# Summing the four strips of a modulation product: transpositions and additions instead of products with a selection matrix

## The chip, the cores and the metric

The kernel runs on one core of a Trainium2 chip. Its engines work beside each other: TensorE (PE in the rows; its loads of the stationary operand are PEld), VectorE (DVE), ScalarE (ACT), GpSimd (POOL) and SyncE (SP), whose queue issues nearly all transfers from device memory. [...] The metric is the device time of one execution in microseconds (us); the kernel before was timed in three runs.

## The reference

One layer of a diffusion backbone, for 512 latent tokens and 128 context tokens that share all weights. What bears on this case is the modulation: a conditioning vector of 1,024 values for each of the two token groups is multiplied by a matrix of 1,024 by 6,144, and the result is six vectors of 1,024 for each group (shift, scale and gate, twice). Everything behind the first norm needs the first two of them.

```python
mod = (jax.nn.silu(cond) @ w_ada + b_ada)[..., None, :]
sh1, sc1, g1, sh2, sc2, g2 = jnp.split(mod, 6, axis=-1)
h = _rmsnorm(x, norm1_g) * (1 + sc1) + sh1
mq, mk, mv, mo, gates, q_lat, kv_lat, k_rope = _split_cols(h @ w_in, IN_SIZES)
...
x = x + g1 * (jnp.concatenate([hm, ha], axis=-1) @ w_out)
h2 = _rmsnorm(x, norm2_g) * (1 + sc2) + sh2
x = x + g2 * (jnp.square(jax.nn.relu(h2 @ w_mlp_up)) @ w_mlp_down)
```

## The kernel before

Tokens lie along the free dimension, 640 of them, features along the 128 partitions. Large products are made in three terms (a high part and a low part of each operand) so that they keep float32 accuracy. Order of the work: norm of x, modulation and the input projection for the values of the first head group (`mv`), key and value latents (`kv`), query latents (`ql`), then per head `qk` and `mo`, the mLSTM, the query up projection (`qu`), the attention, the output projection, and the two feed-forward products, which fill the second half. The order on each engine is set by a scheduler that moves instructions by a timeline of its own, so a changed instruction can move others near it.

The modulation is made in twelve **visits**, each of 512 of the 6,144 columns for both groups. Four (`ada_first`, g from 0 to 3) stand at the start and give shift1 and scale1; eight (`ada_steps`) are spread over the `ql` and `qk` products (visits 5 to 8) and over `qu` (visits 9 to 12), where their weights come in chunks `st` of 1 MB from `in_w_ada`. A chunk has one of two buffers, so SyncE issues the next one when the products of an older one are done.

In a visit, `strips` (line 389) runs 32 products of 32 output rows each, four side by side in the array, one for each strip j. Strip j takes half of the 1,024 inputs (k = j // 2) and half of the columns (n = j % 2); rows 0 and 1 of a strip hold the two groups, the other 30 are zero. So each result is the sum of two strips. `mod_cols` forms that sum and turns it from rows into columns: ScalarE copies the 128 x 256 block out of PSUM (line 394), two products with a 128 x 4 selection matrix of ones and zeros (line 397; the matrix is the last four columns of `small`) sum the strips and move features onto partitions, and two VectorE instructions add the bias and write `modT` (line 400).

`modT` is then read by the norm (lines 475 to 482, per pair of feature blocks: `acol`, `h`, and the high and low parts `hh` and `hl`, which are the operands of `mv`), and later by the second norm and the gates. Near visits 9 to 12 the attention starts: `Tq` and `Tk` (lines 928 and 937) are transpositions of the first head's query and key, `mx` and `mr` (lines 947 and 954) its row maxima and their row, and `st` (line 982) its first scores. Line 488 and its neighbours are the three terms of a product (`mm3`).

Of the kernel before, what the change touches and what calls it, by code (L numbers as in the profile page):

```python
# [14 lines left out]
ALU = mybir.AluOpType  # L15
# [4 lines left out]
P = 128  # L20
# [34 lines left out]
def hybrid_layer(ctx: ExitStack, tc: tile.TileContext, d, o):  # L55
    nc = tc.nc
    V, S, G, PE = nc.vector, nc.scalar, nc.gpsimd, nc.tensor
# [23 lines left out]
    def view(t, off, *shape):  # L81
        n = int(np.prod(shape))
        v = t[:, off:off + n]
        if len(shape) == 1:
            return v
        names = "abcd"[:len(shape)]
        return v.rearrange("p (%s) -> p %s" % (" ".join(names), " ".join(names)), **dict(zip(names, shape)))

    def Tt(name, dt=F32, n=T):
        t = tp.tile([P, 646], dt, tag="t", name=name)  # L90
        return t[:, :n]
# [7 lines left out]
    def psD(name):  # L99
        return psd.tile([P, 1024], F32, tag="d", name=name)  # L100

    def psS(name):
        return pss.tile([P, 512], F32, tag="s", name=name)
# [96 lines left out]
    def wget(key, ahead=3):  # L200
        i = state["get"]
        assert chunks[i][0] == key, (chunks[i][0], key)
        wsplit(i + 1)
        wdma(i + 4)
        wsplit(i + ahead)
        state["get"] += 1
        return ready.pop(i)
# [120 lines left out]
    ident = const.tile([P, P], F32, name="ident")  # L328
# [8 lines left out]
    small = const.tile([P, 98], F32, name="small")  # L337
# [3 lines left out]
    cond, bada = small[:, 25:41], small[:, 41:89]  # L341
# [41 lines left out]
    modT = const.tile([P, 48, 2], F32, name="modT")  # L383

    def strips(ps, n, q, w):

        for j in range(4):
            k, c = j // 2, slice((j % 2) * n, (j % 2) * n + n)
            PE.matmul(ps[32 * j:32 * j + 32, 0:n], lhsT=sz[:, 2 * q + k, :], rhs=w[:, k, c], start=q == 0, stop=q == 3, tile_position=(0, 32 * j))  # L389

    def mod_cols(n, c0, step, ps):

        rows, pt = Tt(f"m4{c0}", n=n), ps[:, 256:512]
        S.copy(rows, ps[:, 0:n])
        nb = n // P
        for m in range(nb):
            PE.matmul(pt[:, m * 4:m * 4 + 4], lhsT=rows[:, m * P:(m + 1) * P], rhs=small[:, 94:98], start=True, stop=True)
        for k in range(2):
            c = slice(c0 + k * step, c0 + k * step + nb)
            V.tensor_tensor(out=modT[:, c, :], in0=pt[:, 0:4 * nb].rearrange("p (m n c) -> p m n c", n=2, c=2)[:, :, k],  # L400
                            in1=bada[:, c].unsqueeze(2).broadcast_to([P, nb, 2]), op=ALU.add)

    fps = {}

    def ada_first(g, q0=0, q1=4):

        if q0 == 0:
            fps[g] = psS(f"ada{g}")
        for q in range(q0, q1):
            strips(fps[g], 256, q, adu[2 * g + q // 2][:, 2 * (q % 2):2 * (q % 2) + 2])  # L410
        if q1 == 4:
            mod_cols(256, 2 * g, 8, fps[g])

    ada_key = iter(ada_order)
    ada_ps = {}

    def ada_steps(n, ahead=3):
        for _ in range(n):
            nb, q = next(ada_key)
            if q == 0:  # L420
                ada_ps[0] = psS(f"ada{nb}")
            w = view(wget(("ada", nb, q), ahead), 0, 2, 2, 512)
            for k in range(2):
                strips(ada_ps[0], 256, 2 * q + k, w[:, k])
            if q == 1:
                mod_cols(256, 4 * nb, 2, ada_ps[0])


    def rstd_bc(pc, name):
# [15 lines left out]
    for k in range(0, KT, 2):  # L445
# [4 lines left out]
        for i in range(NT):  # L450
            c = 5 * k + 2 * i
            PE.matmul(pc[:, c:c + 2], lhsT=sq[0][:, i * P:(i + 1) * P], rhs=mean_col, start=True, stop=True)
    ms1 = sm("ms1", [P, NT], bufs=1)
    V.tensor_reduce(out=ms1, in_=pc[:, 0:5 * KT].rearrange("p (j i b) -> p i b j", i=NT, b=2)[:, :, 0], axis=AX.X, op=ALU.add)
    ada_first(0, 0, 2)
    ada_first(0, 2, 4)
    rb = rstd_bc(ms1, "n1")
    acol1 = const.tile([P, KT, 2], F32, name="acol1")
# [7 lines left out]
    for g in range(4):  # L466
        if g:
            ada_first(g)
        if g == 1:
            rbs = Tt("rb1")  # L470
            S.copy(rbs[:, 0:TL], rb[0])
            S.copy(rbs[:, TL:T], rb[1])
            rb = rbs[:, 0:TL], rbs[:, TL:T]
        c2 = slice(2 * g, 2 * g + 2)
        V.tensor_scalar(out=acol1[:, c2], in0=modT[:, 8 + 2 * g:10 + 2 * g, :], scalar1=1.0, scalar2=None, op0=ALU.add)
        V.tensor_tensor(out=acol1[:, c2], in0=acol1[:, c2], in1=n1g[:, c2].unsqueeze(2).broadcast_to([P, 2, 2]), op=ALU.mult)
        for k in (2 * g, 2 * g + 1):
            h_ = Pp(f"h_{k}")
            for w, (r_, c) in enumerate(zip(rb, (slice(0, TL), slice(TL, T)))):
                V.scalar_tensor_tensor(out=h_[:, c], in0=xk(k)[:, c], scalar=acol1[:, k, w:w + 1], in1=r_, op0=ALU.mult, op1=ALU.mult)  # L480
                S.activation(out=HH[k][:, c], in_=h_[:, c], func=AF.Identity, bias=modT[:, k, w:w + 1])
                V.scalar_tensor_tensor(out=HL[k][:, c], in0=h_[:, c], scalar=modT[:, k, w:w + 1], in1=f(HH[k][:, c]), op0=ALU.add, op1=ALU.subtract)
# [7 lines left out]
    def group_n(keys, kts, ncol, name, nada=0):  # L490
        banks = []
        for j in range(2):
            t = psD(f"{name}_{j}")
            banks += [t[:, 0:512], t[:, 512:1024]]
        banks.append(psS(f"{name}_2"))
        k = 0
        for key, nk in zip(keys, kts):
            hi, lo = wget(key)
            for kk in range(nk):
                for i in range(NT):  # L500
                    c = slice(kk * ncol, (kk + 1) * ncol)
                    mm3(banks[i][:, :ncol], HH[k][:, i * P:(i + 1) * P], HL[k][:, i * P:(i + 1) * P], hi[:, c], lo[:, c], k == 0, k == KT - 1)
                k += 1
                if nada and (k - 1) % (2 // nada) == 2 // nada - 1:
                    ada_steps(1)
        return [b[:, :ncol] for b in banks[:NT]]
# [21 lines left out]
    for i in range(NT):  # L528
# [7 lines left out]
                      in_=st[:, KL + ROPE:KL + ROPE + 8].rearrange("p (a b) -> p a b", a=2))  # L536
        V.tensor_copy(out=gf[:, i, :].rearrange("p (a b) -> p a b", a=2)[:, :, 0:4],
                      in_=st[:, KL + ROPE + 8:KL + ROPE + 16].rearrange("p (a b) -> p a b", a=2))
# [48 lines left out]
    for ci, row in enumerate((r_a, r_e, r_w)):  # L587
        nt = NT if ci < 2 else 4
        pc = psS(f"pcol{ci}")
        for i in range(nt):  # L590
            PE.transpose(out=pc[:, i * 64:(i + 1) * 64], in_=row[:, i * P:(i + 1) * P], identity=ident[0:64, 0:64])
        V.tensor_copy(out=cols[:, ci, 0:nt].rearrange("p t d h -> p (t d) h"),
                      in_=pc[:, 0:nt * 64].rearrange("p (t b) -> p t b", b=32)[:, :, 0:4])
# [8 lines left out]
    for w in range(2):  # L602
# [4 lines left out]
                        in1=gs.unsqueeze(1).broadcast_to([P, NT, 2, 16]), op=ALU.mult)  # L607
# [195 lines left out]
    for k in range(2):  # L803
        pt = psD(f"ckt{k}")
        for i in range(NT):
# [17 lines left out]
                    in0=krn[:, 0:4].rearrange("p t (a b) -> p t a b", a=2)[:, :, ::-1, :],  # L823
                    in1=sg_[:, 1, 0:4].rearrange("p t (a b) -> p t a b", a=2), op=ALU.mult)
# [9 lines left out]
    for hf in range(2):  # L834
# [7 lines left out]
        for i in range(6):  # L842
            ps = psD(f"kvu{hf}{i}")[:, 0:512]
            for k in range(2):
                c = slice(k * 512, (k + 1) * 512)
# [21 lines left out]
    for k in range(3):  # L867
        pt = psD(f"qlt{k}")
# [5 lines left out]
    for hf in range(2):  # L874
# [4 lines left out]
        for i in range(NT):  # L879
            ps = (psS if i % 2 else psD)(f"qu{hf}{i}")  # L880
            for k in range(3):
                hi, lo = w0 if k < 2 else w1
                c = slice((k % 2) * QL, (k % 2) * QL + QL)
# [7 lines left out]
            if i < 4:  # L891
                rt = view(Pp(f"rt{hf}{i}"), 0, 4, ROPE)
                V.tensor_tensor(out=rt.rearrange("p h (a b) -> p h a b", a=2),
                                in0=p4[:, :, NOPE:QK].rearrange("p h (a b) -> p h a b", a=2)[:, :, ::-1, :],
                                in1=sg_[:, 0, i:i + 1, :].rearrange("p t (a b) -> p t a b", a=2).broadcast_to([P, 4, 2, 16]), op=ALU.mult)
# [6 lines left out]
        for k in range(4):  # L902
            G.tensor_tensor(out=qn[:, :, k], in0=qn[:, :, k], in1=rqt[:, :, k:k + 1].broadcast_to([P, NT, QK]), op=ALU.mult)
        qn_u.append(qn)
        ada_steps(4, 3 if hf == 0 else 1)

    mix.append(U("mix1"))
# [153 lines left out]
    for n in range(len(steps) + DN):  # L1061
        if n < len(steps):
# [8 lines left out]
            if (h, j) in MSP:  # L1071

                k = MSP.index((h, j))
# [83 lines left out]
    for m in OUT_ORDER:  # L1157
        if m == 0:
            ps = ps_first
            with tc.issue_after(factors.ins):  # L1160
                mmT(ps, w_first, MHv, MLv, KT, 4)
        elif m == OUT_ORDER[1]:
            ps = psD(f"wo{m}")
# [4 lines left out]
        else:  # L1168
            ps = psD(f"wo{m}")
# [12 lines left out]
        else:  # L1182
            k = m - 4
# [3 lines left out]
            c = TL - HT  # L1187
# [95 lines left out]
    for g in range(NG):  # L1283
# [5 lines left out]
        for i in range(2):  # L1289
            p = 2 * g + i  # L1290
# [12 lines left out]
        for h, m2 in downs(g):  # L1303
            w = wnext(("down", h, m2))
            for m in (2 * m2, 2 * m2 + 1):
                ps = psD(f"dn{h}{m}")
                c = (m % 2) * 512
# [107 lines left out]
```

## Time and profile before

| What | Value |
|---|---|
| time, median of 3 runs | 885.75 us (884.52 to 885.99) |
| the profiled execution's own time | 885.93 us |
| its span, first to last instruction | 883.8 us |
| TensorE busy | 856.6 us, 97% of the span |
| VectorE busy | 615.9 us, 70% |
| ScalarE busy | 436.6 us, 49% |
| GpSimd busy | 297.2 us, 34% |
| chain that ended last, by engine | TensorE 84%, VectorE 8%, DMA 3%, ScalarE 3% |
| mean DMA rate | 101 GB/s |

The span is what the trace covers; 2.1 us of the profiled execution's time lie around it. Busy time counts an engine's instructions, and TensorE's products overlap each other, so their durations don't add up to time: what an instruction costs there is seen in how far the starts of its neighbours are moved apart. The chain that ended last is followed back from the last instruction; an engine's share of it says how much of the span went by while its work was what everything waited for.

### The profile page before, as it was taken

Reading aid. Unit: us, or ns where it says so; the run is one execution under the profiler, and the core shown is the slowest. Engines: PE = TensorE matmul, PEld = TensorE weight load, DVE = VectorE, ACT = ScalarE, POOL = GpSimd, SP = SyncE. Lnnn points to the kernel's source line nnn. Section 1 sums busy time; section 2 is a strip of 40 time slices with the busy share of each in tenths; the row PEclk is TensorE's granted clock in tenths of the full one; section 3 lists DMA queues with packets and bytes.
Section 4 is the critical chain, followed back from the end, with each engine's and each line's share of the span. In section 5 each row is a group of like instructions: output and inputs, shape, how many; then the busy total and the mean of one; then the engine's idle time right before and its main releaser. Section 6 shows DMA issues by size and latency. Waiting matters only on the chain.

```text
span 883.8 us, 15202 instructions
## 1 busy us (share of the span) xinstructions
PE 856.6 (97%) x5805; PEld 801.8 (91%) x5805; DVE 615.9 (70%) x1226; ACT 436.6 (49%) x959; POOL 297.2 (34%) x301
## 2 busy tenths in 40 slices
PE   6999999999889999999989999999999999999998
PEld 5689889999778677889989999999999999999998
DVE  2654733646787889977898587595876949678663
ACT  3424425545864688955557253361544517254540
POOL 3100113322333576743753152241514215152300
PEclk9999999999999999999999999999999999999999
DMA  9742853231316200322141312122122221412132
GB/s 358 307 145 61 281 185 89 63 102 48 99 57 239 96 1 1 120 72 72 49 144 45 99 49 96 49 96 96 49 96 88 80 73 57 134 50 73 48 102 90
DMA packets 22328, 89.63 MB, mean 101 GB/s; under 512 B 3144, under 2 KB 3944, under 8 KB 18928
## 3 DMA queue, kind: packets, MB, share of 16 engines
q1 hardware_dynamic: 19440, 81.95, 26.8%
q0 software_dynamic: 1664, 4.26, 1.7%
q10 hardware_dynamic: 1152, 2.46, 0.7%
q8 instruction: 46, 0.75, 0.4%
q14 instruction: 26, 0.21, 0.1%
HBM read 85.33 MB, written 3.32 MB: 100 GB/s over the span
## 4 chain that ended last, share of the span: by engine, by line
PE 84%; DVE 8%; DMA 3%; ACT 3%; issue 1%; POOL 0%; SPq 0%; DVEq 0%; ACTq 0%; POOLq 0%
PE dn L637 25%; PE qk L637 6%; PE wo L637 5%; PE mo L637 3%; PE ada L389 2%; PE pv L1013 2%; DMA st<-in_w_ada 2%; PE n L702 2%; PE up8M L1235 1%; PE up12M L1235 1%; PE up13M L1235 1%; PE up15M L1235 1%; PE up14M L1235 1%; PE up11M L1235 1%; PE up9M L1235 1%; PE up7M L1235 1%
## 5 line engine op out<-in xcount | busy, mean ns | idle before, releaser
L109 ACT CAST wh<-st 128x1024 fp32r<-128x1024 f32 (+4 forms) x69 | 69.3, 1007 | 101.1 <-PE dn L637 32.9
L1118 DVE SCALAR_TENSOR_TENSOR xr<-dn,modT,xr 128x320 f32<-128x320 f32 x64 | 35.3, 551 | 107.3 <-PE dn L637 107.3
L637 PE MATMUL dn<-fh,wh 128*128 128x320 f32 x448 | 102.7, 310 | 0.2 <-ACT fh L1278 0.2
L110 DVE TENSOR_TENSOR wl<-st,wh 128x1024 fp32r<-128x1024 f32 (+4 forms) x67 | 83.3, 1246 | 27.8 <-ACT wh L109 26.8
L637 PE MATMUL dn<-fh,wl 128*128 128x320 f32 x448 | 102.0, 309 | 0.0
L637 PE MATMUL dn<-fl,wh 128*128 128x320 f32 x448 | 98.7, 309 | 0.0
L109 ACT CAST wu<-S 128x512 fp32r<-128x512 f32 x64 | 38.1, 616 | 98.5 <-issue 92.3
L637 PEld LDWEIGHTS dn<-fh,wh 128*128 128x128 f32 x448 | 74.8, 188 | 2.1 <-PE dn L637 1.6
L637 PEld LDWEIGHTS dn<-fh,wl 128*128 128x128 f32 x448 | 75.0, 188 | 0.0
L637 PEld LDWEIGHTS dn<-fl,wh 128*128 128x128 f32 x448 | 74.1, 188 | 0.0
L1273 POOL TENSOR_TENSOR r<-r,rbs 128x320 f32<-128x320 f32 x32 | 37.4, 1180 | 106.9 <-DVE r L1251 106.9
L110 DVE TENSOR_TENSOR wu<-S,wu 128x512 fp32r<-128x512 f32 x64 | 57.4, 906 | 1.1 <-ACT wu L109 0.9
L1277 ACT ACTIVATE r<-r 128x192 f32<-128x192 f32 (+2 forms) x96 | 40.8, 465 | 26.0 <-DVE r L1251 17.1
L729 POOL TENSOR_TENSOR W<-ngb,mask 128x128 f32<-128x128 f32 x40 | 19.5, 501 | 66.5 <-DVE p L739 33.2
L1280 DVE TENSOR_TENSOR fl<-r,fh 128x320 fp32r<-128x320 f32 x56 | 38.1, 699 | 3.0 <-ACT r L1279 3.0
L1004 POOL TENSOR_TENSOR tot<-tot,p 128x512 f32<-128x512 f32 x24 | 37.2, 1550 | 5.9 <-ACT p L986 3.9
L109 ACT CAST wu<-pair 128x512 fp32r<-128x512 f32 x24 | 14.1, 615 | 43.8 <-PE dn L637 41.6
L110 DVE TENSOR_TENSOR pu<-p,pu 128x512 fp32r<-128x512 f32 x32 | 33.0, 1046 | 2.5 <-ACT pu L109 2.5
L219 POOL TENSOR_TENSOR S<-st,st 128x512 f32<-128x512 f32 x8 | 13.0, 1627 | 60.1 <-DVE wu L110 60.1
L1013 PE MATMUL pv<-pu,v 128*128 128x512 f32 x80 | 29.1, 427 | 2.1 <-DVE pu L110 2.0
L637 PE MATMUL wo<-mh,wh 128*128 128x320 f32 x128 | 29.6, 311 | 0.7 <-DVE xr L1120 0.7
L637 PE MATMUL qk<-hh,wl 128*128 128x320 f32 x128 | 29.9, 312 | 0.0
(487 smaller groups left out, 2437.6 us busy)
## 6 DMA issues: line engine op xcount, KB each, us to landing
st<-in_w_ada SPq DMA_DIRECT2D x16, 1024.0 KB, 5.4
st<-in_w_down SPq DMA_DIRECT2D x32, 512.0 KB, 3.4
ad<-in_w_ada SPq DMA_DIRECT2D x8, 1024.0 KB, 17.2
st<-in_w_up SPq DMA_DIRECT2D x16, 512.0 KB, 3.7
pair<-in_w_up SPq DMA_DIRECT2D x16, 512.0 KB, 4.9
st<-in_w_qko SPq DMA_DIRECT2D x12, 512.0 KB, 3.6
st<-in_w_out SPq DMA_DIRECT2D x8, 512.0 KB, 3.5
x<-in_x SPq DMA_DIRECT2D x4, 640.0 KB, 6.8
```

What stands on the lines that cost most here:

```text
L109: S.copy(hi, src)
L110: return eng.tensor_tensor(out=lo, in0=src, in1=f(hi), op=ALU.subtract)
L389: PE.matmul(ps[32 * j:32 * j + 32, 0:n], lhsT=sz[:, 2 * q + k, :], rhs=w[:, k, c], start=q == 0, stop=q == 3, tile_position=(0, 32 * j))
L637: PE.matmul(out[:, hf * 512:hf * 512 + HT], lhsT=wt[:, c], rhs=xt[k][:, hf * HT:(hf + 1) * HT], start=k0 == 0 and n == 0, stop=k1 == nk an ...
L729: G.tensor_tensor(out=W[:, dg:dg + P], in0=nb_[dr][:, j * P:(j + 1) * P], in1=mask[:, dr, :], op=ALU.add)
L1004: G.tensor_tensor(out=tot[h], in0=first, in1=pj, op=ALU.add)
L1013: PE.matmul(pacc[h], lhsT=v_u[hf][:, j, hh_, :], rhs=w, start=j == 0 and k == 0, stop=j == 4 and k == 1)
L1118: V.scalar_tensor_tensor(out=xr[m][:, 0:HT], in0=ps[:, 0:HT], scalar=modT[:, gi_ + m, 0:1], in1=xr[m][:, 0:HT], op0=ALU.mult, op1=ALU.add)
L1235: PE.matmul(ps, lhsT=w[:, c], rhs=b[k], start=k == 0 and w is hi and b is bh, stop=k == 3 and w is lo)
L1273: E.tensor_tensor(out=t, in0=t, in1=rbs[:, c], op=ALU.mult)
L1277: S.activation(out=t[:, c0:c1], in_=t[:, c0:c1], func=AF.Relu, bias=r[n][:, w:w + 1])
L1280: V.tensor_tensor(out=FL[n][:, c], in0=t, in1=f(FH[n][:, c]), op=ALU.subtract)
```

## The change

`mod_cols` transposes the copied block, 128 columns at a time, with the identity matrix (`ident`) in TensorE's transpose form. The strips then lie side by side on the free dimension, 128 x 256 in PSUM, and VectorE sums them: for each half n of the columns one instruction adds strip k = 0 to the bias, and one adds strip k = 1 to what the first wrote. The selection matrix is no longer read (it stays in `small`), and the argument `n`, always 256, is gone. Lines behind `mod_cols` have numbers higher by two.

```diff
--- before.py
+++ after.py
@@ -388,17 +388,19 @@
             k, c = j // 2, slice((j % 2) * n, (j % 2) * n + n)
             PE.matmul(ps[32 * j:32 * j + 32, 0:n], lhsT=sz[:, 2 * q + k, :], rhs=w[:, k, c], start=q == 0, stop=q == 3, tile_position=(0, 32 * j))
 
-    def mod_cols(n, c0, step, ps):
-
-        rows, pt = Tt(f"m4{c0}", n=n), ps[:, 256:512]
-        S.copy(rows, ps[:, 0:n])
-        nb = n // P
-        for m in range(nb):
-            PE.matmul(pt[:, m * 4:m * 4 + 4], lhsT=rows[:, m * P:(m + 1) * P], rhs=small[:, 94:98], start=True, stop=True)
+    def mod_cols(c0, step, ps):
+
+
+        rows, pt = Tt(f"m4{c0}", n=256), ps[:, 256:512]
+        S.copy(rows, ps[:, 0:256])
+        for m in range(2):
+            PE.transpose(out=pt[:, m * P:(m + 1) * P], in_=rows[:, m * P:(m + 1) * P], identity=ident)
+        parts = pt.rearrange("p (m k n c) -> p n m k c", m=2, k=2, n=2)
         for k in range(2):
-            c = slice(c0 + k * step, c0 + k * step + nb)
-            V.tensor_tensor(out=modT[:, c, :], in0=pt[:, 0:4 * nb].rearrange("p (m n c) -> p m n c", n=2, c=2)[:, :, k],
-                            in1=bada[:, c].unsqueeze(2).broadcast_to([P, nb, 2]), op=ALU.add)
+            for n in range(2):
+                c = slice(c0 + n * step, c0 + n * step + 2)
+                V.tensor_tensor(out=modT[:, c, :], in0=parts[:, n, :, k, 0:2],
+                                in1=modT[:, c, :] if k else bada[:, c].unsqueeze(2).broadcast_to([P, 2, 2]), op=ALU.add)
 
     fps = {}
 
@@ -409,7 +411,7 @@
         for q in range(q0, q1):
             strips(fps[g], 256, q, adu[2 * g + q // 2][:, 2 * (q % 2):2 * (q % 2) + 2])
         if q1 == 4:
-            mod_cols(256, 2 * g, 8, fps[g])
+            mod_cols(2 * g, 8, fps[g])
 
     ada_key = iter(ada_order)
     ada_ps = {}
@@ -423,7 +425,7 @@
             for k in range(2):
                 strips(ada_ps[0], 256, 2 * q + k, w[:, k])
             if q == 1:
-                mod_cols(256, 4 * nb, 2, ada_ps[0])
+                mod_cols(4 * nb, 2, ada_ps[0])
 
 
     def rstd_bc(pc, name):
```

The scheduler also moves neighbours of the exchanged instructions, in the `mv` and `kv` products, in `ql` and `qk` (where the two instructions of a visit stand up to three products away from their old place) and around visits 9 to 12; GpSimd's order is as before, and SyncE's differs by one exchanged pair of transfers. Three places are shown. First VectorE at visit 1 (`ms` belongs to the norm of x, `h` is the normed x). Before:

```order
L431 TENSOR_SCALAR ms<-ms_188 128x5
L400 TENSOR_TENSOR modT<-ada_190,small 128x4 x2
L475 TENSOR_SCALAR acol_224<-modT 128x4
L476 TENSOR_TENSOR acol_224<-acol_224,small 128x4
L480 SCALAR_TENSOR_TENSOR h_231<-x_107,acol_224,n_pb_217 128x512
```

After:

```order
L433 TENSOR_SCALAR ms<-ms_188 128x5
L402 TENSOR_TENSOR modT<-ada_190,small 128x4 x2
L402 TENSOR_TENSOR modT<-ada_190,modT 128x4 x2
L477 TENSOR_SCALAR acol_226<-modT 128x4
L478 TENSOR_TENSOR acol_226<-acol_226,small 128x4
L482 SCALAR_TENSOR_TENSOR h_233<-x_107,acol_226,n_pb_219 128x512
```

Two instructions became four, and the last two read `modT`, which the first two write.

Second, TensorE at visit 4, inside the products of `mv` (wl and wh are the low and high part of the weights). Before:

```order
L487 MATMUL mv_366<-wl_377,hh_226 128x512
L488 MATMUL mv_366<-wh_376,hl_228 128x512
L486 MATMUL mv_366<-wh_376,hh_226 128x512
L397 MATMUL ada_326<-small,m_343 128x4 x2
L487 MATMUL mv_366<-wl_377,hh_226 128x512
L488 MATMUL mv_366<-wh_376,hl_228 128x512
L487 MATMUL mv_367<-wl_377,hh_226 128x512
```

After:

```order
L488 MATMUL mv_373<-wh_384,hh_228 128x512
L488 MATMUL mv_374<-wh_384,hh_228 128x512
L488 MATMUL mv_375<-wh_384,hh_228 128x512
L397 MATMUL ada_332<-ident,m_349 128x128 x2
L489 MATMUL mv_373<-wl_385,hh_228 128x512
L490 MATMUL mv_373<-wh_384,hl_230 128x512
L488 MATMUL mv_373<-wh_384,hh_228 128x512
```

The visit's two instructions stand eight products earlier in the change (21 products of `mv` lay between the strips and them, now 11), and of the nine `kv` products that stood behind this place as a block, one now stands ahead of the next six `mv` products, seven behind those, and one later still.

Third, TensorE at visits 11 and 12, where `ada` are the strips, `st` their chunks of weights and `qu`, `Tq`, `Tk`, `mx`, `mr` as named above. Before, where the strips of visit 11 begin:

```order
L488 MATMUL qu_3101<-wh_3021,qtl 128x384
L389 MATMUL ada_3153<-st_3019,sz 32x256 x8
L389 MATMUL ada_3153<-st_3040,sz 32x256 x2
L486 MATMUL qu_3119<-wh_3007,qth 128x384
L487 MATMUL qu_3119<-wl_3008,qth 128x384
```

and, after nine products of `qu`:

```order
L487 MATMUL qu_3119<-wl_3022,qth 128x384
L488 MATMUL qu_3119<-wh_3021,qtl 128x384
L389 MATMUL ada_3153<-st_3040,sz 32x256 x6
L928 MATMUL Tq_3209<-ident,qn_2865 96x128 x5
L397 MATMUL ada_3153<-small,m_3172 128x4 x2
L937 MATMUL Tk_3218<-ident,kn_2615 96x128 x6
L389 MATMUL ada_3178<-st_3042,sz 32x256 x8
L947 MATMUL mx_3229<-qk_3206 128x320 x2
L947 MATMUL mx_3233<-qk_3206 128x320 x2
L389 MATMUL ada_3178<-st_3044,sz 32x256 x8
L947 MATMUL mx_3237<-qk_3206 128x320 x2
```

After, where the nine products of `qu` end:

```order
L490 MATMUL qu_3139<-wh_3039,qtl 128x384
L389 MATMUL ada_3173<-st_3037,sz 32x256 x8
L389 MATMUL ada_3173<-st_3060,sz 32x256 x8
L930 MATMUL Tq_3233<-ident,qn_2881 96x128 x5
L939 MATMUL Tk_3242<-ident,kn_2631 96x128 x6
L397 MATMUL ada_3173<-ident,m_3192 128x128 x2
L949 MATMUL mx_3253<-qk_3230 128x320 x2
L389 MATMUL ada_3200<-st_3062,sz 32x256 x8
L949 MATMUL mx_3257<-qk_3230 128x320 x2
L949 MATMUL mx_3261<-qk_3230 128x320 x2
L956 MATMUL mr_3269<-kc,nm 1x128
L949 MATMUL mx_3265<-qk_3230 128x320 x2
```

In the change the nine `qu` products stand ahead of all sixteen strips of visit 11, the strips are no longer in two pieces, and the last eight strips of visit 12 stand behind all four `mx` and two of the four `mr`. The two instructions of `mod_cols` stand behind `Tk` at visit 11; at visit 12 they stand behind the second head's `Tk`, where before they stood ahead of its `Tq`.

## Rows read from the trace of the kernel before

**Rows 1.** The page's head: span; busy time, share and instructions by engine.

```profile
span 883.8 us, 15202 instructions
...
PE 856.6 (97%) x5805; PEld 801.8 (91%) x5805; DVE 615.9 (70%) x1226; ACT 436.6 (49%) x959; POOL 297.2 (34%) x301
```

**Rows 2.** Windows, 34 to 42 us: busy PE, PEld, DVE, ACT, POOL; PEclk, DMA share, GB/s.

```profile
34.00:42.00 8.00, 8.00 (x58) 5.52 (x59) 4.79 (x12) 2.68 (x5) 0.00 (x0) 1.00 0.50 204
```

**Rows 3.** Records on tile ada: duration ns min/median/max, first and last start.

```profile
L397 PE MATMUL ada<-small,m x48: 167/252/273, 22.3 to 296.8; 128*128 128x4 f32 x48
...
L400 DVE TENSOR_TENSOR modT<-ada,small x24: 148/152/164, 23.0 to 297.8; 128x4 f32<-128x4 f32 x24
```

**Rows 4.** Timeline of TensorE, third visit: start us, us, engine, line, instruction.

```profile
37.03 0.40 PE L487 MATMUL mv<-wl,hh 128*128 128x512 f32 x1
...
37.26 0.50 PE L397 MATMUL ada<-small,m 128*128 128x4 f32 x4
...
37.95 0.39 PE L486 MATMUL mv<-wh,hh 128*128 128x512 f32 x1
```

**Rows 5.** Timeline of TensorE around one transposition between other products.

```profile
303.36 0.46 PE L947 MATMUL mx<-qk 96*128 96x320 f32 x2
...
303.65 0.27 PE L972 MATMUL co<-ident,pc 128*128 128x128 f32 x1
...
303.68 0.54 PE L947 MATMUL mx<-qk 96*128 96x320 f32 x2
...
304.05 0.63 PE L1013 MATMUL pv<-pu,v 128*128 128x512 f32 x2
```

**Rows 6.** Timeline of the first visit; in brackets idle time before, and releaser.

```profile
16.44 3.64 PE L389 MATMUL ada<-ad,sz 128*32 128x256 f32 x32
...
22.30 0.56 PE L397 MATMUL ada<-small,m 128*128 128x4 f32 x4
...
22.79 1.93 PE L389 MATMUL ada<-ad,sz 128*32 128x256 f32 x32
...
22.97 0.23 DVE L400 TENSOR_TENSOR modT<-ada,small 128x4 f32<-128x4 f32 x2 [6.04 <-PE ada L397]
...
25.20 0.50 PE L486 MATMUL mv<-wh,hh 128*128 128x512 f32 x1 [0.47 <-ACT hh L481]
```

**Rows 7.** Timeline of VectorE: small instructions, each reading the one before.

```profile
280.79 0.18 DVE L372 SCALAR_TENSOR_TENSOR rqt<-nwt,rqt 128x20 f32<-128x20 f32 x1
...
281.00 0.18 DVE L370 TENSOR_TENSOR nwt<-rqt 128x20 f32<-128x20 f32 x1
```

**Rows 8.** Timeline between the fifth and the sixth visit.

```profile
97.34 1.22 DVE L110 TENSOR_TENSOR wl<-st,wh 128x1024 fp32r<-128x1024 f32 x1
...
99.01 0.38 SPq L177 DMA_DIRECT2D st<-in_w_ada  x1
...
104.89 1.05 PE L389 MATMUL ada<-st,sz 128*32 128x256 f32 x10 [0.72 <-DMA st<-in_w_ada]
```

**Rows 9.** Chain that ended last, 283 to 300 us: start us, us, what.

```profile
283.05 0.79 PE ada L397 x8
...
285.69 1.42 PE ada L389 x20
...
289.91 4.69 DMA st<-in_w_ada
...
296.24 0.84 DVE nm L948
...
299.41 0.47 PE st L982
```

**Rows 10.** The last two transfers: SyncE's issues, us to landing; a window as in rows 2.

```profile
286.75 3.48 SPq L177 DMA_DIRECT2D st<-in_w_ada  x2
...
st<-in_w_ada SPq DMA_DIRECT2D x2, 1024.0 KB, 4.7
...
292.00:293.00 1.00, 0.86 (x17) 0.30 (x7) 0.93 (x5) 0.78 (x2) 0.00 (x0) 1.00 1.02 434
```

## The prediction

> **What bounds the kernel now.** I read the page's head first: TensorE is busy for 856.6 of 883.8 us, 97% [rows 1]. So a change pays by what it takes off TensorE, or off one of the few waits that leave TensorE idle, and the question at each of the twelve visits is which of the two holds there. The window of 34 to 42 us, with two visits in it, shows TensorE busy for 8.00 of 8.00 us while VectorE is busy for 4.79 [rows 2]: there its queue is the bound, and VectorE has room. The timeline then gives three kinds of visits. Visits 2 to 4 and 6 to 10 lie inside a queue of other products; the third is shown [rows 4]. Visit 1 is a chain: TensorE stands idle for 0.47 us until `hh`, made from its result, is there [rows 6]. Visits 11 and 12 lie where the chain that ended last runs through a transfer of weights, VectorE and ScalarE [rows 9]. The sums are made against the profiled execution, 885.93 us (span 883.8 and 2.1 around it); it lies 0.18 us above the median of the three runs.
>
> **The selection products and what replaces them.** A visit has two such products, 48 records in twelve visits, so two records for a product [rows 3]. What they cost TensorE is seen in their neighbours' starts: from the product before (37.03) to the second one behind (37.95) are 0.92 us, of which the two ordinary products take 0.23 each (37.03 to 37.26) [rows 4]. That leaves 0.46 us for four records, 0.11 each. Visits 9 and 10 agree: eight records hold the chain for 0.79 us and move the next product by a further 0.1 [rows 9].
>
> A transposition of the same shape in the same engine is there, as one record: two `mx` products normally stand 0.29 us apart from the next pair (303.36 to 303.65), and with a transposition ahead of them the next work starts at 304.05, 0.40 after 303.65. So it costs 0.11 us [rows 5]. Two of them cost 0.22, in place of 0.46, and I take 0.23 us off a visit. The bounds: two in a row between products of another shape might cost up to 0.33 (0.12 saved); the saving can't pass the 0.46 that is there. I stay near the first, since one record at 0.11 is the price on both sides.
>
> **Visits 2 to 4**: 3 x 0.23 = 0.69 us, in a queue that has no idle time [rows 2]. The longer VectorE part (below) is hidden there, because other products, the next visit's strips among them, stand in the queue ahead of those that need `hh` and `hl`. At visit 4 the transpositions come eight products (1.9 us) earlier and the `kv` products move; all of it is the same work in another order in a full queue, so 0.
>
> **Visit 1.** Transpositions end 0.22 us sooner. The additions go the other way: the two before take 0.23 us together [rows 6] at 0.152 each [rows 3], so the second starts 0.08 after the first. The added two read what the first two write, and in such a chain VectorE starts an instruction 0.21 us after the one that it reads (280.79 to 281.00) [rows 7]. So the third starts at 0.21 instead of ending the group at 0.23; the four end 0.21 us later than two did (0.29 if the third waits for the second). Net -0.01 to +0.07; I take 0. [...]
>
> **Visit 5**: 0. Its saving meets a wait: the products of the next chunk wait 0.72 us for the transfer [rows 8]. SyncE issues that transfer at 99.01, behind another that waits for the buffer which the VectorE instruction at 97.34 frees; that one ends a chain of scans, which begins ahead of visit 5. Bounds 0 to -0.23. **Visits 6 to 8**: again in a full queue of `ql` and `qk`, 3 x 0.23 = 0.69. **Visits 9 and 10**: 0.45 of the 0.89 of [rows 9].
>
> **Visits 11 and 12.** The exchange itself is hidden; the order decides. Before, 20 records of strips (1.42 us, from 285.69) stood ahead of nine `qu` products and 12 behind, and SyncE issued the last two chunks at 286.75 and 289.90 [rows 10], as the strips freed their buffers. The second took 4.69 us and held the chain to 294.60 [rows 9]. In the change the nine products come first, which takes 1.6 us at 0.18 each, and the 32 records of strips then take 1.9 [rows 6], so they end near 289.1, with one switch between shapes less. The first chunk is issued near 288.2, the second near 289.1. A chunk alone takes 4.7 us [rows 10]. Unhindered the second lands at 293.8; if it can only follow the first, whose 1 MB lands at 292.9, it comes at about 295.3 (1 MB at the 434 GB/s that such a transfer reached takes 2.4 us [rows 10]). I take the later one. Behind it, the chain before went: 16 records, 1.07 us; two `mx`; a VectorE maximum of 0.84 at 296.24; `mr`, `Tq`, two ScalarE copies; scores at 299.41 [rows 9], 4.8 us after landing. Now the `mx` and two `mr` are done ahead of the last strips, so only strips, `Tq` and the copies remain: 4.8 less 0.5 for the `mx` and 0.9 for the maximum, 3.4 us, which gives 298.7. The fourth maximum may still be late, so I take 0.5 us off and not 0.7. Bounds: -1.3 (no hindrance), +0.4 (chunks slow each other more, or the added additions in VectorE's queue, which wait for the transpositions, delay the copies).
>
> **Sum**: 0.69 + 0 + 0 + 0.69 + 0.45 + 0.5 = 2.3 us. 885.93 - 2.3 = 883.6 on the profiled execution, 883.5 on the median.
>
> **The rivals.**
> *A pair of transpositions is dearer* (0.33): 8 visits save 0.12 each, with the order 1.5 us in all: 884.3. For it: only single transpositions between products are shown [rows 5]. Chance 0.15.
> *The last two chunks hinder each other* and the reordering loses 0.3 us: -1.8 + 0.3, again 884.3. For it: both are now issued within 1 us of each other, before 3.15 [rows 10]; against it: less work lies behind the landing. 0.17.
> *More than forecast*: the second chunk lands unhindered and visit 5's saving stays: -1.8 - 1.3 - 0.2 = -3.3, 882.5. 0.12.
> *Slower*: TensorE's pace at the start. [...] 0.07. Other losses, among them a wait in the reordered `kv` products: 0.04.
> The forecast keeps 0.45, with a range of its own of 882.9 to 884.1.
>
> **How the numbers follow.** A measurement of this kernel tells about 0.2%, 1.8 us, from no change: faster means below 884.0. The forecast lies there in nine of ten of its cases: 0.45 x 0.9 + 0.12 = 0.53. The same: 0.15 + 0.17 and the rest of the forecast, 0.36. Slower: 0.11. The range leaves out the slow cases and part of the third rival: 881.9 to 886.2.
>
> **What would show it.** Right: records at line 397 fall from 48 to 24, neighbours of a visit stand 0.23 us closer; the first `mv` product starts within 0.1 of 25.20; the wait before the strips of visit 6 grows by 0.2; the first scores start about 2.3 us sooner, near 297.1, and everything behind moves with them. Wrong: the 1.8 us are not there at 285 us (the transposition's price); the last chunk lands later than 295 less the gain so far, or VectorE stands between `Tq` and the copies (the order); strips at 22 us still take 3.6 us (the pace).

## The result, and the profile after

The changed kernel takes 889.88 us (median of six runs, 888.95 to 892.57); the kernel before, run beside it, 885.71 us. The ratio is 1.0053, with a 95% interval of 1.0035 to 1.0071: slower by 4.2 us, where 883.5 was forecast. The profiled execution took 892.57 us, the longest of the six, with a span of 890.8. Its page's head answers to [rows 1]:

```profile
span 890.8 us, 15169 instructions
...
PE 857.7 (96%) x5781; PEld 802.4 (90%) x5781; DVE 618.2 (69%) x1250; ACT 436.6 (49%) x959; POOL 296.7 (33%) x301
```

The work itself is as forecast: 24 matmul records fewer, 24 additions more. TensorE's timeline of the third visit answers to [rows 4]: from the product ahead of the transpositions to the second product behind them it is now 36.55 to 37.23, 0.68 us, where it was 0.92. A visit saves 0.24 us, for 0.23 forecast.

```profile
36.55 0.39 PE L489 MATMUL mv<-wl,hh 128*128 128x512 f32 x1
36.78 0.38 PE L397 MATMUL ada<-ident,m 128*128 128x128 f32 x2
36.91 0.48 PE L490 MATMUL mv<-wh,hl 128*128 128x512 f32 x1
37.23 0.40 PE L488 MATMUL mv<-wh,hh 128*128 128x512 f32 x1
```

The loss lies in three other places. The first is visit 6. SyncE's and TensorE's timelines answer to [rows 8]: the chunk is issued 0.88 us sooner (98.13, before 99.01), but the issue itself takes 1.32 us instead of 0.38, and the strips start at 106.22, later than before; TensorE waits 3.17 us for the chunk, before 0.72.

```profile
98.13 1.32 SPq L177 DMA_DIRECT2D st<-in_w_ada  x1
...
106.22 1.14 PE L389 MATMUL ada<-st,sz 128*32 128x256 f32 x12 [3.17 <-DMA st<-in_w_ada]
```

Windows of one us (columns as in [rows 2]; the third number from the end is the granted clock) show what follows the wait: the clock goes from 1.00 to 0.50 and is back at 1.00 only within the window from 110. The last two rows are the third place, at 462 us. There TensorE had been idle three times within some 6 us (1.83, 0.93 and 0.69 us), around the second norm; before it idles there much the same (1.60, 0.95 and 0.71 us), and the clock stays full (1.00).

```profile
106.00:107.00 1.00, 0.78 (x12) 0.39 (x12) 0.00 (x0) 0.00 (x0) 0.50 (x2) 1.00 1.05 438
107.00:108.00 1.00, 1.00 (x8) 0.38 (x6) 0.00 (x0) 0.00 (x0) 0.19 (x1) 0.53 0.99 418
108.00:109.00 1.00, 1.00 (x5) 0.19 (x5) 0.98 (x5) 0.00 (x0) 0.00 (x0) 0.50 0.96 388
110.00:111.00 1.00, 1.00 (x7) 1.00 (x6) 0.14 (x2) 0.00 (x0) 0.00 (x0) 0.76 0.91 259
...
462.00:463.00 1.00, 1.00 (x6) 1.00 (x5) 0.93 (x2) 0.00 (x0) 0.00 (x0) 0.53 0.00 0
468.00:469.00 1.00, 1.00 (x6) 1.00 (x5) 1.00 (x2) 0.00 (x0) 0.70 (x1) 0.56 0.00 0
```

The second place is visits 11 and 12, in the chain that ended last (compare [rows 9]). The 32 strips stand together, as the order said; the last chunk takes 7.20 us from issue to landing (before 4.69; the expectation of the first run below calls it the second last by mistake), and the scores start at 302.87. From this chunk's issue to the scores it is 10.49 us, before 289.91 to 299.41, 9.50.

```profile
290.46 1.91 PE ada L389 x32
...
292.38 7.20 DMA st<-in_w_ada
...
299.63 1.07 PE ada L389 x16
...
302.15 0.58 ACT qk L957
...
302.87 0.47 PE st L984
```

So this execution has lost 3.2 us against before at the tenth last `qu` product, the last point ahead of the exchanged order (288.54, before 285.36), 3.5 by the scores, and 7.0 at the end of the span; the last 3.5 are the half clock from 462 to 469, which by an estimate (TensorE busy throughout, at half the pace) costs half of its 6.8 us. At the end of visit 11's strips the loss reads 2.5 us (292.38 against 289.91), because the new order, with one switch between shapes less, reaches that end 0.7 us sooner (nine `qu` products and 32 strips take 1.58 and 1.91 us, before 1.77 and, in two pieces, 1.42 and 1.01).

### The profile page after: what moved, and what is told of

The parts are those of the page before. It is cut to its first block, busy times and chain, and to the rows that moved or that the text cites. A ratio compares the mean times of both kernels' runs of the same rounds, so it can differ in the third digit from the quotient of the medians.

```text
span 890.8 us, 15169 instructions
## 1 busy us (share of the span) xinstructions
PE 857.7 (96%) x5781; PEld 802.4 (90%) x5781; DVE 618.2 (69%) x1250; ACT 436.6 (49%) x959; POOL 296.7 (33%) x301
## 4 chain that ended last, share of the span: by engine, by line
PE 84%; DVE 7%; DMA 4%; ACT 3%; issue 2%; POOL 0%; SPq 0%; DVEq 0%; POOLq 0%; ACTq 0%
PE dn L639 25%; PE qk L639 6%; PE wo L639 5%; PE mo L639 3%; DMA st<-in_w_ada 3%; PE ada L389 2%; PE pv L1015 2%; PE up1M L1237 2%; PE n L704 2%; PE up12M L1237 1%; PE up8M L1237 1%; PE up4M L1237 1%; PE up9M L1237 1%; PE up5M L1237 1%; PE up11M L1237 1%
## 5 line engine op out<-in xcount | busy, mean ns | idle before, releaser
L639 PE MATMUL qk<-hl,wh 128*128 128x320 f32 x128 | 30.7, 316 | 0.0
```

The costliest lines, as they stand in the source:

```text
L639: PE.matmul(out[:, hf * 512:hf * 512 + HT], lhsT=wt[:, c], rhs=xt[k][:, hf * HT:(hf + 1) * HT], start=k0 == 0 and n == 0, stop=k1 == nk an ...
```

## The experiments

Twelve runs; each ratio is to the kernel before on the same chip, with its 95% interval. They were made on three chips in groups of four, in the order shown. The one table that they all feed, on visit 6, stands behind them.

**The change once more.** No edit.

> The changed kernel once more, as it is, for a second trace. Theory 1 (the losses are the kernel's own): the same three places again: TensorE waits about 3 us for the chunk of weights ahead of the strips of visit 6 (0.7 before), with its clock at half for about 3 us behind that wait; the second last chunk takes about 7 us to land and the first scores start about 3.4 us late; and the clock is at half for about 6 us near 462 us. Time 889 to 892. Rival (chance of the one profiled run): at least one of the two stretches at half clock is gone, the place of visit 6 costs under 1 us, and this execution is 887 to 889.

1.0033 (1.0015 to 1.0051). The place of visit 6 is there again (issue 0.95 us, wait 2.95 us, clock at half behind it); the half clock near 462 is not, but one stands from 297 to 304 us instead. So visit 6 belongs to the kernel, and the third place comes and goes.

**The change split by visits.** The function chooses by its arguments; in the visits that the tuple lists it keeps the old body.

```
+        if (c0, step) in (...):
+            pt = ps[:, 256:512]
+            for m in range(2):
+                PE.matmul(pt[:, m * 4:m * 4 + 4], lhsT=rows[:, m * P:(m + 1) * P], rhs=small[:, 94:98], start=True, stop=True)
...
+            return
```

> Transpositions and four additions in visits 1 to 4 alone, the selection product in visits 5 to 12. Forecast's steps: 0.7 to 0.9 us gained by visit 5, kept or swallowed by the wait at visit 6: 885.0 to 885.7. Theory 'sooner work meets the transfer of visit 6 worse': the gain is there at the strips of visit 5, but the chunk for visit 6 takes 8 us instead of 5.8, TensorE waits 3 us, its clock falls, and 2.5 us are lost there: 887 to 888. Theory 'the transpositions of visits 5 to 10 themselves do it': nothing lost at visit 6, 885.

1.0027 (1.0008 to 1.0046). What the theory of sooner work describes is there: the issue takes 1.43 us, the strips wait 2.65 us, and the clock is at half from 106 to 112. Whether sooner work is the cause is tested further down.

> Transpositions in visits 5 to 10 alone; TensorE's order behind visit 10 is that of the change (all strips of visit 11 behind the products qu). Forecast's steps: 0.69 + 0.45 + 0.5 gained, 884.1. Theory 'the order at visits 11 and 12': gains 0.9 by visit 10, then loses 1.0 us against before between the strips of visit 11 and the first scores, because the second last chunk is issued later and takes 7 us: 885.8. Theory 'the transpositions themselves lower the clock': the half clock at visit 6 is here too, 2.5 us lost there: 888.

1.0015 (0.9997 to 1.0033). Issue 0.38 us, wait 0.84, clock full until the last 3 us of the profiled execution. From the first `mv` product to the end of visit 11's strips it is 1.33 us faster than before, but part of that is the new order. To the tenth last `qu` product, ahead of the exchanged order, it is 259.56 us, before 260.15: 0.59 gained for 1.14 forecast. The waits for chunks near 104, 116 and 275 us are 0.84, 0.34 and 0.64 us, before 0.72, none and 0.47, 0.63 more in sum. So TensorE gains what was forecast, and half of it goes into waits. From the strips' end to the scores it is 10.55 us, where before took 9.54; from the tenth last `qu` product 14.34, before 14.05. The order loses 0.3 us where a gain of 0.5 was forecast.

> Transpositions in visits 11 and 12 alone; the strips of visit 11 stand as before (20 ahead of the products qu). Theory 'order': nothing lost at the chunks, 885.4 to 885.8, scores within 0.3 us of before. Theory 'the additions delay the chain there': the scores start 0.3 to 0.6 us later than before, 886.2. In both the clock near 460 us stays full; if it is at half there, that fall belongs to the length of what lies ahead or to chance, not to transpositions ahead of 280 us.

0.9982 (0.9965 to 1.0000). With the old order of the strips, the scores follow them by 8.63 us, 0.9 less than before (13.14 from the tenth last `qu` product, before 14.05); within 0.3 of before was expected. The additions delay nothing there. The chain:

```profile
288.77 1.01 PE ada L389 x12
289.80 4.86 DMA st<-in_w_ada
...
298.39 0.47 PE st L993
```

**SyncE's order.** What do transpositions in visits 1 to 4 do to a transfer at 98 us? In SyncE's queue the change swaps one pair of issues, the last `kv` chunk and a chunk of visit 5. One kernel puts that swap into the kernel before, one takes it out of the version of visits 1 to 4.

```
+            if key == ("kv", 2):
+                early = [ada_dma(j) for j in range(i, i + 4) if chunks[j][0][0] == "ada"]
...
+                with tc.issue_after(early[1].ins):
+                    nc.sync.dma_start(out=t[:, :n], in_=ap)
```

> The kernel before, selection products everywhere, TensorE's order untouched; SyncE issues the second chunk of visit 5 one place ahead of the last kv chunk instead of one behind, as in the change. Theory 'SyncE's order': the chunk of visit 6 takes 7.7 to 8 us instead of 5.8, TensorE waits about 2 to 3 us for it instead of 0.7, its clock falls behind that wait, and the median is 887.5 to 889 with nearly every execution at a mean clock of 0.996 or less. Rival 'sooner work' (the transfer is met 0.9 us earlier by the same neighbours): nothing changes here, wait 0.7 us, 885.7 to 887.

0.9998 (0.9980 to 1.0017): issue 0.38, wait 0.56. The swap does nothing.

```
+                if key == ("ada", 4, 1):
+                    with tc.issue_after(kv2[0].ins):
+                        nc.sync.dma_start(out=t[:, :n], in_=ap)
```

> Transpositions in visits 1 to 4 with TensorE's order of that version, but SyncE keeps the order of before (last kv chunk ahead of the second chunk of visit 5). Theory 'SyncE's order': the chunk of visit 6 is back at about 5.8 us, TensorE waits 0.7 to 1.6 us, no fall of the clock there, 885 to 886.5. Rival 'sooner work': 7.7 to 8 us and a wait of 2.6 us again, 888.

1.0053 (1.0033 to 1.0074): issue 1.12, wait 2.62. My theory of SyncE's order has fallen, from both sides. This kernel and that of visits 1 to 4 differ only by the swap and read 1.0053 and 1.0027 on two chips, with intervals that overlap: a single ratio here tells little below 0.002, and the argument rests on the traces.

**The order of visit 11.**

```
         for i in range(NT):
+            if hf == 1 and i == 4:
+                ada_steps(1, 1)
...
+                with tc.issue_after(last_strips[-7].ins) if (hf, i) == (1, 4) else contextlib.nullcontext():
                     mm3(ps[:, 0:QL], qth[:, k, i * P:(i + 1) * P], qtl[:, k, i * P:(i + 1) * P], hi[:, c], lo[:, c], k == 0, k == 2)
...
-        ada_steps(4, 3 if hf == 0 else 1)
+        ada_steps(4 - hf, 3 if hf == 0 else 1)
```

> The change, with the first chunk of visit 11 put ahead of the last nine products qu, so that the first of the last two chunks is issued some 1.6 us ahead of the second, as before, and not within 1 us. The place of visit 6 is left as in the change. Theory 'order at visits 11 and 12': from the end of the strips of visit 11 to the first scores 9.5 to 9.9 us instead of 10.5, the second chunk lands in about 5.5 us, no long wait and no fall of the clock near 295; 1 to 2 us faster than the change, 888.3 to 889. Rival: the chunk still takes 7 us, 890.

1.0023 (1.0004 to 1.0042). Strips to scores: 9.30 us instead of 10.55; visit 6 is bad as in the change (wait 2.68).

> The change with both orders put back: SyncE's of r6 and the first chunk of visit 11 of r7. If the two orders are all that the change lost by: 2.3 us of the forecast without the reordering's 0.5, so 1.8 faster than before, 884 to 885.5, and mean clocks like those of before. If the transpositions themselves lower the clock: 888 or more, clocks of 0.995.

1.0032 (1.0011 to 1.0053), with clocks of 0.995 in the mean: what I expected if the transpositions themselves cost. But visit 6 was bad again (issue 1.49, wait 3.55), and the kernel of visits 5 to 10 had transpositions without that; the clock fell once more at 354 us in this trace. Strips to scores: 9.97 us.

**Instruction fetch.** The symptom that comes first in every bad trace is SyncE's long issue (0.95 to 1.49 us, in the good ones 0.38 or 0.39). Among the transfers around it one differs in place: a packet of 16 KB on a queue that the profile calls instruction. One window each of the kernel before (97 to 98 us) and of the change (97.5 to 98.5), in 40 slices of 0.025 us: the packet is the 9. It starts at 97.40 before, 1.6 us ahead of the issue at 99.01, and at 97.83 in the change, 0.3 ahead of the issue at 98.13. Its share of 16 engines' time, 7.8% of one us, makes it 1.25 us long, so it lies across the issue; before, with 6.0%, it is 0.96 us long and over ahead of it.

```profile
DMA  0000000000000000900000000000000000000000
...
q8 instruction: 1, 0.02, 6.0%
```

```profile
DMA  0000000000000900000000000000000000000000
...
q8 instruction: 1, 0.02, 7.8%
```

A selection product is four TensorE instructions (two loads, two products), a transposition two: by the pages 5,805 products and as many loads before, 5,781 of each in the change, for 24 exchanged. Five visits of the change have 20 fewer by then. If the packet brings TensorE's instructions, a fetch comes later in the program by as many. What a packet carries no view shows; the counts fit that reading. The kernel before has 46 such packets for 11,610 TensorE instructions, 252 for each. And the packet in question starts when TensorE has started the same number of instructions, 1,169 to 1,175 in all fourteen traces, whatever was added or removed ahead of it. Windows from the start to the packet, of the kernel before and of the kernel further down from which 20 instructions are removed (the first two brackets count products and loads):

```profile
0.00:97.41 97.41, 88.54 (x586) 74.15 (x587) 49.41 (x118) 36.09 (x64) 12.82 (x20) 1.00 0.60 224
...
0.00:98.08 98.08, 87.32 (x584) 72.88 (x585) 51.01 (x121) 36.44 (x64) 12.85 (x20) 1.00 0.60 223
```

So I added 20 instructions to the change (five products whose results nobody reads), and in the kernel before removed 20.

```
     pc = psS("n1_pc")
+    for i in range(5):
+        PE.matmul(pc[:, 400:404], lhsT=ident, rhs=small[:, 94:98], start=True, stop=True)
```

> The change with five extra selection products (20 TensorE instructions, results unused) among the first sums, at 8 to 16 us, as many as its first five visits have fewer. Theory 'instruction fetch': in all six traces with a slow transfer at visit 6 the instruction queue's packet of 16 KB starts within 0.5 us ahead of SyncE's issue of that chunk, and SyncE's issue takes 0.95 to 1.5 us; in the four with a fast one it starts 1.6 us ahead, and the issue takes 0.38. With the stream as long as before, the packet is back 1.6 us ahead, the issue takes 0.38, the chunk 5.7 to 6.2 us, TensorE waits 0.6 to 1.6 us, its clock stays full there, and the median is 1.5 to 3 us below the change's, near 886.5 to 888. Rival 'sooner work': the wait of 2.6 to 3.5 us and the fall of the clock stay, 889 to 891.

1.0005 (0.9985 to 1.0025), from 1.0033 and 1.0053 of the change. The packet is back at 1.64 us ahead, and the clock stays full there; it falls twice later in this trace, at 292 and 456 us. Timelines of SyncE and TensorE:

```profile
98.30 0.38 SPq L177 DMA_DIRECT2D st<-in_w_ada  x1
...
104.09 0.42 PE L389 MATMUL ada<-st,sz 128*32 128x256 f32 x4 [0.85 <-DMA st<-in_w_ada]
```

```
-        for i in range(NT):
+        for i in range(NT if k else 0):
...
-    V.tensor_reduce(out=ms1, in_=pc[:, 0:5 * KT].rearrange(
+    V.tensor_reduce(out=ms1, in_=pc[:, 10:5 * KT].rearrange(
```

> The kernel before without the first five of the twenty products that sum squares for the first norm (20 TensorE instructions fewer at 8 us; the mean leaves out a quarter of the features, so the output differs); no transposition in a visit, every order as before. Theory 'instruction fetch': the packet of 16 KB moves to within 0.5 us of SyncE's issue, the issue takes about 1 us or more, the chunk 7.5 to 8 us, TensorE waits 2.5 to 3.5 us, its clock falls for 3 to 7 us: 888 to 890, clocks of 0.996 or less in nearly all executions. Rival (the transpositions or the sooner work make it): nothing changes, 885.5 to 887.

1.0052 (1.0033 to 1.0071). This kernel leaves out the first five of the twenty products that sum squares for the first norm, so its output is not the reference's. Work is taken away from the kernel before, no visit is touched, and it is as slow as the change. It also settles the rival of sooner work: the chunk is issued at 98.23 us here and at 98.30 with 20 added, with opposite ends. Timelines, and a window behind the wait:

```profile
98.23 1.31 SPq L177 DMA_DIRECT2D st<-in_w_ada  x1
...
106.64 1.49 PE L389 MATMUL ada<-st,sz 128*32 128x256 f32 x9 [3.27 <-DMA st<-in_w_ada]
```

```profile
107.00:108.00 1.00, 1.00 (x10) 0.35 (x2) 0.00 (x0) 0.00 (x0) 0.55 (x1) 0.50 0.98 414
```

**Repaired versions.** The edits are those above, put together.

> Transpositions in visits 1 to 8 and 11, 12, selection products in 9 and 10, so that the strips of visit 11 stand as before; four extra selection products at the start keep the instruction stream's length. If fetch and order are the two losses: visits 1 to 4 gain 0.7 to 0.9 (some of it into the wait at visit 6), 6 to 8 0.7, visits 11 and 12 0.9 (as in the run of visits 11 and 12 alone): 2 us faster than before, ratio 0.9965 to 0.999. If the transpositions themselves cost or lower the clock: same as before or slower.

0.9996 (0.9978 to 1.0013), slower than the 0.9965 to 0.999 expected. Visit 6 (issue 0.38, wait 1.11) and strips to scores (8.67 us) are as expected, and the profiled span is 882.7; seven of twelve executions still have a mean clock of 0.996 or less.

> The change with both repairs: five extra products at the start, and the first chunk of visit 11 ahead of the last nine products qu. If fetch and order explain the loss: no slow transfer at visit 6, strips of visit 11 to first scores 9.3 to 9.6 us, 884 to 885.5, clocks like those of before. If not: 888 or more.

0.9988 (0.9970 to 1.0005), median 885.19 beside 885.98: the change with both repairs, where the change itself has 1.0053 and 1.0033. The wait at visit 6 is 1.70 us, from strips to scores 8.90 (9.3 to 9.6 expected). This one and that of visits 11 and 12 alone are the fastest here; neither interval lies clear of 1.

All fourteen traces at visit 6 (packet: how long ahead of SyncE's issue it starts, read in slices of 0.025 us; the time to the strips is from that issue):

| kernel | TensorE instructions by then | packet ahead | issue took | to the strips | TensorE waited | clock behind it |
|---|---|---|---|---|---|---|
| before | 0 | 1.60 | 0.38 | 5.88 | 0.72 | full |
| visits 5 to 10 | -4 | 1.56 | 0.38 | 5.77 | 0.84 | full |
| visits 11, 12 | 0 | 1.72 | 0.38 | 6.20 | 1.04 | full |
| before, SyncE swapped | 0 | 1.62 | 0.38 | 5.73 | 0.56 | full |
| change, 20 added | 0 | 1.64 | 0.38 | 5.79 | 0.85 | full |
| visits 1-8, 11, 12, 16 added | -4 | 1.50 | 0.38 | 6.04 | 1.11 | full |
| change, both repairs | 0 | 1.71 | 0.39 | 6.62 | 1.70 | full |
| change | -20 | 0.28 | 1.32 | 8.09 | 3.17 | half |
| change again | -20 | 0.43 | 0.95 | 7.86 | 2.95 | half |
| visits 1 to 4 | -16 | 0.28 | 1.43 | 7.80 | 2.65 | half |
| the same, SyncE kept | -16 | 0.44 | 1.12 | 7.78 | 2.62 | half |
| change, first chunk early | -20 | 0.35 | 1.03 | 7.59 | 2.68 | half |
| change, both orders | -20 | 0.29 | 1.49 | 8.48 | 3.55 | half |
| before, 20 fewer | -20 | 0.15 | 1.31 | 8.41 | 3.27 | half |

## Why the prediction was wrong

**The step that failed** is the one for visit 5 and the wait behind it. I took the transfer's 5.84 us as fixed and let only its issue move, so the worst that I saw was a saving swallowed by the wait (bounds 0 to -0.23). In its place the runs showed a transfer that takes 2 us longer. The cause is not where the work is exchanged but the length of TensorE's instruction stream: with 16 or 20 instructions fewer the packet that follows their count, which I read as a fetch of them, starts 0.15 to 0.44 us ahead of the issue of the chunk, instead of 1.50 to 1.72. Shown by the pair that moves the stream without touching a visit, in both directions: 20 instructions added take the slow transfer out of the change (1.0005), 20 removed bring it into the kernel before (1.0052). The price in the change's profile: 3.17 instead of 0.72 us of wait, 2.45, and, as an estimate, half of the 3.4 us at the low clock (a transposition took 0.42 to 0.48 us there, at the full clock 0.27), 1.7, together 4.2 us; with the low clock for 6.8 us, as in the kernel of visits 1 to 4, 1.93 and 3.4, 5.3.

How the packet delays the chunk is not settled, and a packet close ahead is not enough. Behind the first 30 us, the fourteen traces have 92 issues on SyncE's queue with a 16 KB instruction packet starting 0.1 to 0.8 us ahead. Of these, 31 follow another issue within 0.9 us, as the chunk of visit 6 does (0.42), and 30 of the 31 took 0.66 to 1.52 us; the other 61 took no more than 0.33. Two of the 30 stand in the kernel before (0.79 us at 268.44, 1.52 us at 555.83). TensorE did not stop for the packet: its products are busy for all of the 1.30 us from 97.80 to 99.10 in the change, and for all of the 1.00 us from 97.40 before. The data transfer next to it took longer, 8.0 us from issue to landing, before 5.8.

**The clock.** The slow case (0.07) put its loss at the start, in TensorE's pace. That transpositions could slow it no run shows; in its place the strips behind visit 1 took 1.93 us as before (22.34), and the window of 22 to 25 us reads a clock of 1.00 in both kernels. The clock fell elsewhere, at the end of waits or just behind them: at visit 6 in all seven traces in which TensorE waited 2.6 us or more there, in none of the seven with 1.7 or less. One of the seven has no transposition in a visit, so the falls need none.

**Price of a pair**: right, 0.24 us for 0.23 a visit. **Visit 1**: right. The first `mv` product came 0.26 us sooner, outside the 0.1 that I named, but so did the transpositions, behind other products; from them to that product it is 2.91 us (22.03 to 24.94), before 2.90, and the additions' two pairs start 0.20 us apart, for 0.21 forecast. **Visits 2 to 4**: from the first `mv` product to the issue ahead of visit 6, 73.19 us instead of 73.81, 0.62 gained for 0.69; the nine traces with transpositions there read 73.13 to 73.20, the other five 73.78 to 73.82. **Visits 6 to 10**: 0.59 us for 1.14 in the kernel of visits 5 to 10, and 0.63 more in longer waits for chunks, so the price is right and the waits, which I counted at visit 5 alone, took half. In the change the waits for chunks at 277 and 279 us (0.51 and 1.38 us, before 0.47 in all) take 1.4; why the chunk issued at 269.73 took 7.0 us there (before 4.8) stays open.

**Visits 11 and 12**: the order is as read, and what lies behind the last landing takes 3.29 us (299.58 to 302.87), for 3.4. Counted from the tenth last `qu` product, ahead of the exchanged order, the scores follow after 14.33 us in the change and 14.34 in the kernel of visits 5 to 10, before after 14.05: 0.3 us lost where 0.5 gained was forecast, which is the price of the rival with the two chunks and inside my bound of 0.4. Mis-sized was the transfer: I took the slower of two cases, 6.2 us from issue to landing; it took 7.20, and 6.6 in visits 5 to 10. But that alone does not make the loss. A term that I put at nothing is the path from the first of the two chunks: I called the `mx` and two `mr` done ahead of the last strips, but they wait for the first chunk's strips and for VectorE's maximum, and the last strips stand behind them in TensorE's queue. In the chain of visits 5 to 10 this path ends last:

```profile
287.48 5.04 DMA st<-in_w_ada
292.56 1.07 PE ada L389 x16
...
294.16 0.84 DVE nm L959
...
295.66 1.00 PE ada L389 x16
...
298.83 0.47 PE st L993
```

From the first chunk's landing (292.52) to the last strips it is 3.14 us; the last chunk, issued at 288.34, had landed 0.7 us ahead of them. In the change the two paths end together, and TensorE waits only 0.15 us for the last chunk:

```profile
299.63 1.07 PE L389 MATMUL ada<-st,sz 128*32 128x256 f32 x16 [0.15 <-DMA st<-in_w_ada]
```

With the forecast's own landing of the first chunk, 292.9, the term gives 292.9 + 3.14 + 3.4 = 299.4 instead of 298.7: no gain. Wrong too was that the exchange itself is hidden: with the old order it gains 0.9 us (13.14 in visits 11 and 12 alone, 13.18 in the first repaired version). The first chunk alone ahead of the `qu` products brings 14.33 to 13.51 (13.10 with both repairs, 14.18 in the change with both orders). So the order it is. In two of the four traces with all 32 strips together the clock fell there as well (from 291.9 and from 297.3 us, for 6.8 us each), in none of the ten others.

**The third place** is not the change's own. The clock fell between 452 and 469 us in five of fourteen traces, one of them the kernel before with SyncE's pair swapped, whose TensorE, VectorE and ScalarE run the same instructions in the same order as the kernel before:

```profile
456.00:457.00 1.00, 1.00 (x8) 1.00 (x7) 1.00 (x4) 0.04 (x1) 0.00 (x0) 0.86 0.00 0
457.00:458.00 1.00, 1.00 (x6) 1.00 (x5) 0.45 (x1) 0.00 (x1) 0.00 (x0) 0.50 0.00 0
```

What decides it in one execution and not in the next stays open. It weighs on every median here: of 102 executions of the kernel before, 33 have a mean clock of 0.996 or less, with spans up to 6 us above the mean of the others (890.0 against 884.0 in the first group). Whether the repaired versions meet it more often (7 of 12 and 2 of 12) can't be told from so few.

So the price that makes up the 1.8 us forecast ahead of visit 11 is there, and what ate it is above all a transfer that I took to be independent of the number of TensorE's instructions. The profiled execution adds up, as an estimate from its rows. Lost are 4.2 us at visit 6 and 1.4 in the waits at 277 and 279 us; gained are 2.2 in nine visits and 0.3 at the start. That makes 3.1 lost, for 3.2 read at the tenth last `qu` product; then come 0.3 by the order and 3.4 by the third place. With fetch and order repaired, the change is 0.8 us faster than before by the medians, which its interval does not set apart from no change.

## What to carry to other kernels

Where the path waits for a transfer with little to spare, its duration is a term of the sum with its own bounds, even if the edit doesn't touch it; ask what else is on the DMA engines at its issue, the instruction queue included: here 16 or 20 TensorE instructions fewer ahead of it brought its packet from 1.50 to 1.72 us ahead of the issue to 0.15 to 0.44. A slow version with a long issue row is worth one run with padding: a few idle products at the start moved nothing here (first strips at 16.38 us, before 16.44) and tell a change's own cost from where the packets fall. And a wait can cost twice, by itself and by the clock behind it: at visit 6 it did when it had grown from 0.6 to 1.7 us to 2.6 or more.

## What was not expected of the hardware

A packet of 16 KB on the instruction queue, starting 0.15 to 0.44 us ahead of the issue of a 1 MB transfer at visit 6, went with an issue of 0.95 to 1.49 us instead of 0.38 and a time to its first use of 7.6 to 8.5 us instead of 5.7 to 6.6; 1.5 us ahead it did not. That transfer is issued 0.42 us behind another. A 1 MB transfer issued alone, 2.8 us behind the one ahead of it, took 0.33 us to issue and 4.7 to land with such a packet 0.39 us ahead of it (266.19 us, the kernel before with SyncE's pair swapped). At visit 6 TensorE's clock fell to 0.50 in every trace with a wait of 2.6 us or more, for 3.4 or 6.8 us, though the engine was busy again at times between 0.9 us ahead of the fall and 0.5 us behind it.
